# When attention's rows of weights begin, and when Q and K are loaded

## The chip, the cores and the metric

The kernel runs on one core of a Trainium2 chip. A core has TensorE (PE: matrix products and transposes, with its weight loads shown apart as PEld), VectorE (DVE), ScalarE (ACT), GpSimd (POOL) and SyncE (SP, which here issues all DMA transfers); each works off its own queue in order. The metric is the time on the device in microseconds, as the median over runs.

## The reference

One layer of a streaming encoder with 1024 tokens and 1024 channels, in float32. A combined projection gives Q, K and V for 8 heads of softmax attention and 8 heads of stick-breaking attention, and two gates. Each branch is projected, gated and summed; an output projection, a LayerNorm, a SwiGLU block of width 2816 and a second LayerNorm follow. What matters here is the attention:

```python
# a: softmax over own chunk and 8 previous ones (64 queries each), with a bias by distance
scores = einsum('bcqhd,bckhd->bhcqk', qc, kb) / sqrt(dh) + bias
out = einsum('bhcqk,bckhd->bcqhd', softmax(scores), vb)
# b: stick-breaking, strictly causal, 128 queries at a time
log_keep = where(causal, log_sigmoid(-z), 0.0)
suffix = cumsum(log_keep, axis=3, reverse=True) - log_keep
w = exp(where(causal, log_sigmoid(z) + suffix, -inf))
out = einsum('bhqs,bshd->bqhd', w, v)
```

Tokens are stored in reverse order, so that a query block's keys are its own block and those with higher numbers.

## The kernel before, in words

The stages come one after another: the combined projection, attention, the second branch's output projection and gating, the output projection with the first LayerNorm, and the two halves of the feed-forward block with the second LayerNorm. A matrix product in full precision is made of three products of rounded parts (a high part and the rest), which is why a tensor is "split" in many places: ACT writes the high part, DVE subtracts (lines 108 and 109).

Attention goes head by head, eight a heads (softmax, `br` 0), then eight b heads (stick-breaking, `br` 1). The queries of a head are eight blocks of 128, numbered 0 to 7, in two groups of four.

A **row** of weights is the work on one query block (a "unit" in the code). In an a head (`soft_block`) PE makes the scores, in pieces of up to 512 keys on two `sc` banks; DVE adds the bias and takes the minimum (line 492), ACT the exponential (497), DVE the reciprocal (499) and POOL the scaling (500). The rows of an a head reach over 5, 5, 5, 5, 4, 3, 2, 1 blocks of keys. In a b head (`stick_block`) ACT takes two sigmoids of each piece of scores (525, 526), DVE forms running products by scans (529, 533) and POOL multiplies (535). Its rows reach over 8, 7, 6, 5, 4, 3, 2, 1 blocks.

A **step** is one block of keys of one group: eight steps for the first group of a head and four for the second, twelve in all. In a step PE transposes the weights of that block for the queries of the group (the "turn", line 556) into one of three `tr` banks (in b heads one of the three holds an auxiliary tile, `ident_ps`, for the scans), ACT and DVE split them into `pt`, and two steps later (`LAG = 2`) PE multiplies them with V into the one `pv` bank (569, 570). After a group's last product ACT copies one half of the bank to `yt` and DVE adds the other (575, 576); only then can the next group's first product begin.

Between these, `fill_until` puts products of other work: gate projections (418) and the first branch's output projection (603), 18 products of 512 columns for each a head and 42 for each b head, spread over the twelve steps.

In the order in which the program is written, `LEAD[pos]` says how many rows, counted from the current head's first (eight per head), have begun by step `pos`; they are issued ahead of the step's turn. Before, the same twelve numbers held for both kinds of head. The head's Q and K (five transfers, in a heads also the bias row, an ACT pass and two small POOL writes) are loaded by `load_qk`, V by `load_v`; each has slots for two heads. At build time a planner orders each engine's instructions: by the order of the program, but what is not ready by its own costs gives way to later work that is. The order on the chip is the planner's and then fixed.

Of the kernel before, what the change touches and what calls it, by code (L numbers as in the profile page):

```python
# [31 lines left out]
LO, HI = slice(0, HW), slice(HW, 2 * HW)  # L32


LAG = 2
LEAD = (5, 6, 6, 7, 8, 8, 9, 10, 10, 11, 12, 13)

FILL = (18.0, 42.0)

# [7 lines left out]
def hybrid_trunk_kernel(ctx: ExitStack, tc, x, xt, w_in, b_gate, rel_bias, w_proj,  # L47
# [14 lines left out]
    def slot(tag, name, dtype=F32):  # L62
        return pool.tile([P, 1024], dtype, tag=tag, name=name, bufs=SLOTS[tag])
# [371 lines left out]
    def load_qk(hd):  # L435

        i, h = hd["i"], hd["h"]
        n = 2 * i + h
        q, k = (d[i][h * P:(h + 1) * P] for d in (q_dr, k_dr))
        for key, part in (("qs", None), ("kh", 0), ("kl", DH)):  # L440
            t = hd[key] = slot(key, f"{key}{n}", F32R)
            if part is None:
                dma(t.bitcast(F32), q)
            else:
                for half in (slice(0, DH), slice(DH, P)):
                    dma(t[half].bitcast(F32), k[part:part + DH])
        if hd["br"] == 0:
            hd["bias"] = rel_bias_tile(hd["n"])

    def load_v(hd):  # L450

        n = 2 * hd["i"] + hd["h"]
        t = slot("v", f"v{n}", F32R)
        dma(t.bitcast(F32), v_dr[n])
        hd["v"] = t.rearrange("p (t c) -> p t c", t=8)
# [16 lines left out]
    def rel_bias_tile(head):  # L472
        braw = slot("kp", f"braw{head}")
        src = rel_dr[head:head + 1, 0:640]
        dma(braw[:, 0:640],
            bass.AP(tensor=src.tensor, offset=src.offset, ap=[[1, P], [1, 640]]))
        bias = slot("kp", f"bias{head}")
        nc.scalar.activation(bias[:, 0:640], braw[:, 0:640][:, ::-1], AF.Copy, scale=-1.0)  # L478
        nc.gpsimd.memset(bias[0:DH, 576:640], BIG)  # L479
        nc.gpsimd.memset(bias[DH:P, 0:DH], BIG)  # L480
        return bias
# [158 lines left out]
    def fill_until(t):  # L640
        while state["t"] < t and not state["done"]:
            try:
                state["t"] += next(fill)
            except StopIteration:
                state["done"] = True


    heads = []
# [12 lines left out]
    wunits, vsteps = [], []  # L661
# [12 lines left out]
    wi = 0  # L674
# [2 lines left out]
    nhead = 12  # L677
    goal = 0.0
    load_qk(heads[0])
    load_v(heads[0])  # L680
    for si, (hd, g, st, box) in enumerate(vsteps):
        hidx, pos = si // nhead, si % nhead
        if hidx < 15 and pos == 1:
            load_qk(heads[hidx + 1])
        if hidx < 15 and pos == 4:
            load_v(heads[hidx + 1])
        while wi < min(hidx * 8 + LEAD[pos], len(wunits)):
            wunits[wi]()
            wi += 1
        if st == 0:  # L690
            steps_of[(hidx, g)] = value_steps(hd, g, box)
        turn, mult = steps_of[(hidx, g)][st]
        turn()
        last = goal
        goal += FILL[hd["br"]] / nhead
        fill_until(0.5 * (last + goal))
        pend.append(mult)
        if len(pend) > LAG:
            pend.pop(0)()
        fill_until(goal)  # L700
# [361 lines left out]
```

## Time and profile before

| | |
|---|---|
| median of 3 runs | 1499.21 us (1498.03 to 1502.22) |
| profiled execution | 1501.38 us |
| its span, first to last instruction | 1499.3 us |
| PE busy | 1440.3 us (96%) |
| DVE busy | 1043.9 us (70%) |
| ACT busy | 679.7 us (45%) |
| POOL busy | 282.4 us (19%) |
| granted TensorE clock, mean | 0.993 |

The profile gives, for one execution, each engine's busy time, the instructions in order of time with the idle time before each and what ended it, and sums of those waits. In a line of the timeline the first two numbers are start and length in microseconds, then engine, source line, operation, output and inputs; "x2" means that two neighbours of the same kind are merged. In a line of waits the numbers are the total in microseconds, how often, and the longest.

### The profile page before, as it was taken

How to read it: one execution, taken by the hardware profiler on the slowest of the kernel's cores; microseconds unless marked ns; L12 is line 12 of the kernel's file. 1: busy time of each engine (PE TensorE's matmuls, PEld its weight loads, DVE VectorE, ACT ScalarE, POOL GpSimd, SP SyncE). 2: the span in 40 equal slices, each digit the busy share in tenths (PEclk: the TensorE clock that was granted, in tenths of full speed). 3: DMA queues.
4: the chain of work that ended last, by engine and by line, in shares of the span. 5: the costliest groups of instructions: out<-in, count | busy, mean ns of one | idle time of the engine just before them, and what ended most of it. 6: DMA issues, size and time to landing. Idle time of an engine off the chain costs nothing. (4 is left out here: it accounts for less than half of the span.)

```text
span 1499.3 us, 19075 instructions
## 1 busy us (share of the span) xinstructions
PE 1440.3 (96%) x6728; PEld 1179.6 (79%) x6728; DVE 1043.9 (70%) x1702; ACT 679.7 (45%) x1174; POOL 282.4 (19%) x322
## 2 busy tenths in 40 slices
PE   8999999999999999899999899999999998999997
PEld 6788888887887777777787688888888886778886
DVE  8865556435878887887849966767777755767757
ACT  6444444336877778775303534444444433111201
POOL 0000000004344558650014000000000003341016
PEclk9999999999999999999999999999999999999999
DMA  6555555247754556647502123444444456677602
GB/s 211 163 175 169 168 168 170 98 144 213 206 170 142 159 165 204 187 157 280 183 0 87 62 100 121 152 155 155 155 155 154 155 189 232 245 249 267 234 8 105
DMA packets 81215, 244.05 MB, mean 163 GB/s; under 512 B 10064, under 2 KB 10064, under 8 KB 81120
## 3 DMA queue, kind: packets, MB, share of 16 engines
q1 hardware_dynamic: 81120, 242.84, 48.5%
q8 instruction: 53, 0.87, 0.2%
q14 instruction: 42, 0.34, 0.1%
HBM read 162.03 MB, written 80.77 MB: 162 GB/s over the span
## 5 line engine op out<-in xcount | busy, mean ns | idle before, releaser
L535 POOL TENSOR_TENSOR w_b<-w_b,kp_b 128x511 f32<-128x511 f32 (+3 forms) x96 | 97.5, 1021 | 51.5 <-DVE kp_b L533 40.6
L950 POOL TENSOR_TENSOR tda<-wdR,wdL 128x512 f32<-128x512 f32 x8 | 10.7, 1340 | 491.6 <-DMA wdR<-in_w_ffn_out_dram 477.8
L533 DVE TENSOR_TENSOR_SCAN kp_b<-kp_b,ident_ps 128x384 f32<-128x384 f32 (+6 forms) x88 | 78.3, 890 | 4.1
L479 POOL MEMSET bias<- 64x64 f32 x8 | 1.2, 146 | 334.5 <-ACT bias L478 334.5
L745 POOL TENSOR_TENSOR mv<-mv,neghalf 128x1 f32<-128x1 f32 x16 | 23.9, 1495 | 211.4 <-DVE mv L744 211.4
L525 ACT ACTIVATE kp_b<-sc_b 128x512 f32<-128x512 f32 (+3 forms) x96 | 48.5, 505 | 31.4 <-PE sc_b L462 26.5
L183 DVE TENSOR_TENSOR c<-sxp,c 128x512 f32<-128x512 f32 x16 | 11.1, 692 | 73.9 <-issue 40.7
L925 DVE TENSOR_TENSOR x<-dx,x 128x512 f32<-128x512 f32 x64 | 43.6, 689 | 24.6 <-PE dx L995 24.6
L109 DVE TENSOR_TENSOR pt_b<-tp_b,pt_b 128x512 fp32r<-128x512 f32 (+1 forms) x96 | 51.1, 543 | 10.9 <-ACT pt_b L108 10.4
L170 PE MATMUL szf<-x1S63h,wcf 128*128 128x512 f32 x176 | 57.8, 389 | 0.0
L500 POOL TENSOR_SCALAR w_a<-w_a,st_a 128x640 f32<-128x640 f32 (+2 forms) x64 | 42.6, 671 | 67.2 <-DVE st_a L499 49.6
L556 PE MATMUL tp_b<-ident,w_b 128*128 128x128 f32 x288 | 49.3, 277 | 5.2 <-DVE pt_b L109 2.8
L108 ACT CAST pt_b<-tp_b 128x512 fp32r<-128x512 f32 (+1 forms) x96 | 47.1, 497 | 13.7 <-PE tp_b L556 13.2
L109 DVE TENSOR_TENSOR sl<-h,sl 128x512 fp32r<-128x512 f32 x56 | 38.4, 686 | 20.2 <-ACT sl L108 20.2
L108 ACT CAST sl<-h 128x512 fp32r<-128x512 f32 x56 | 34.8, 621 | 35.6 <-PE syf L170 17.1
L109 DVE TENSOR_TENSOR pt_a<-tp_a,pt_a 128x512 fp32r<-128x512 f32 (+1 forms) x96 | 45.5, 484 | 7.6 <-ACT pt_a L108 7.3
L497 ACT ACTIVATE w_a<-w_a,st_a 128x640 f32<-128x640 f32 (+2 forms) x64 | 44.6, 698 | 12.8 <-DVE st_a L492 11.2
L118 PE MATMUL ops<-wh_o,ml 128*128 128x512 f32 x128 | 50.2, 392 | 0.2 <-DVE ml L109 0.2
L115 PE MATMUL ops<-wh_o,mh 128*128 128x512 f32 x128 | 50.2, 392 | 0.0
L116 PE MATMUL ops<-wl_o,mh 128*128 128x512 f32 x128 | 49.9, 390 | 0.0
L556 PE MATMUL tp_a<-ident,w_a 128*128 128x128 f32 x240 | 44.8, 277 | 5.0 <-POOL w_a L500 2.4
L833 ACT ACTIVATE h<-sxf 128x512 f32<-128x512 f32 x22 | 13.2, 598 | 79.6 <-PE sxf L170 79.6
(1881 smaller groups left out, 4833.4 us busy)
## 6 DMA issues: line engine op xcount, KB each, us to landing
s_dr<-sl SPq DMA_DIRECT2D x112, 256.0 KB, 2.2
sd<-s_dr SPq DMA_DIRECT2D x56, 512.0 KB, 5.2
wLf<-in_w_ffn_in_dram SPq DMA_DIRECT2D x22, 512.0 KB, 4.4
wRf<-in_w_ffn_in_dram SPq DMA_DIRECT2D x22, 512.0 KB, 3.6
wLp<-in_w_in_dram SPq DMA_DIRECT2D x17, 512.0 KB, 5.3
wRp<-in_w_in_dram SPq DMA_DIRECT2D x17, 512.0 KB, 4.0
v_dr<-v SPq DMA_DIRECT2D x16, 512.0 KB, 4.3
qs<-q_dr SPq DMA_DIRECT2D x16, 512.0 KB, 6.2
```

The costliest lines, as they stand in the source:

```text
L108: nc.scalar.copy(dst_h, src)
L109: nc.vector.tensor_tensor(dst_l, src, dst_h.bitcast(F32), ALU.subtract)
L115: mm(acc, lh, rh, start=(i == 0), stop=False)
L116: mm(acc, lh, rl, start=False, stop=False)
L118: mm(acc, ll, rh, start=False, stop=(i == n))
L170: mm(acc, lw[:, ks], rx, start=(first and kt == i == 0), stop=(kt == 3 and i == 2), skip_group_check=not first)
L497: nc.scalar.activation(s[:, 0:w], s[:, 0:w], AF.Exp, bias=st[:, m:m + 1], scale=-1.0, accum_out=st[:, 2:3])
L525: nc.scalar.activation(kp[:, c0:e], sc[:, 0:n], AF.Sigmoid, scale=-1.0)
L533: nc.vector.tensor_tensor_scan(kp[:, s0:e], kp[:, s0:e], ident_ps()[:, 0:e - s0], kp[:, s0 - 1:s0], ALU.mult, ALU.bypass)
L535: nc.gpsimd.tensor_tensor(be[:, m0:e], be[:, m0:e], kp[:, m0 - 1:e - 1], ALU.mult)
L556: tr(tp[:, (qb - lo_q) * P:(qb - lo_q + 1) * P], wt[qb - q0][:, (kb - qb) * P:(kb - qb + 1) * P], ident)
L925: nc.vector.tensor_tensor(dst, acc, dst, ALU.add)
```

## The change

The one list of twelve numbers becomes one list for a heads and one for b heads, chosen by the current head's kind. Counted in steps of a head, the rows of a head that begin in the head before (the first group's four and the first ones of the second) and in the head itself move as follows:

| row (block of queries) | 0 | 1 | 2 | 3 | 4 | 5 | 6 | 7 |
|---|---|---|---|---|---|---|---|---|
| begins before | step 6 of the head before | 7 | 9 | 10 | 11 | step 1 of its own head | 3 | 4 |
| now, under an a head | 2 | 4 | 6 | 8 | 10 | step 0 of its own head | 1 | 2 |
| now, under a b head | 2 | 4 | 6 | 8 | 10 | 11 of the head before | step 0 of its own head | 1 |

`load_qk` is written at step 8 for the head after the next, where it stood at step 1 for the next head; the second head's load moves ahead of the first head's `load_v`.

```diff
-LEAD = (5, 6, 6, 7, 8, 8, 9, 10, 10, 11, 12, 13)
+LEAD = ((6, 7, 9, 9, 10, 10, 11, 11, 12, 12, 13, 13), (7, 8, 9, 9, 10, 10, 11, 11, 12, 12, 13, 14))
 ...
     load_qk(heads[0])
+    load_qk(heads[1])
     load_v(heads[0])
     for si, (hd, g, st, box) in enumerate(vsteps):
         hidx, pos = si // nhead, si % nhead
-        if hidx < 15 and pos == 1:
-            load_qk(heads[hidx + 1])
+        if hidx < 14 and pos == 8:
+            load_qk(heads[hidx + 2])
         if hidx < 15 and pos == 4:
             load_v(heads[hidx + 1])
-        while wi < min(hidx * 8 + LEAD[pos], len(wunits)):
+        while wi < min(hidx * 8 + LEAD[hd["br"]][pos], len(wunits)):
             wunits[wi]()
             wi += 1
```

## The prediction

> **What bounds the kernel now.** I read the page's totals first, then busy time by stage, then the waits of TensorE (PE), then one head in order of time on PE, VectorE (DVE) and ScalarE (ACT).
>
> ```profile
> span 1499.3 us, 19075 instructions
> PE 1440.3 (96%) x6728; PEld 1179.6 (79%) x6728; DVE 1043.9 (70%) x1702; ACT 679.7 (45%) x1174; POOL 282.4 (19%) x322
> ```
>
> PE is busy 96% of the span, so the change can win only what PE idles in the stage it touches. Attention is that stage: softmax heads (called a) from 347.5 to about 474 us, stick-breaking heads (b) to 690. Columns: length of the stretch, then busy time of each engine.
>
> ```profile
> core 0: us, PE busy (x) PEld busy (x) DVE busy (x) ACT busy (x) POOL busy (x), PEclk, DMA share, GB/s
> 347.50:474.00 126.50, 120.62 (x732) 102.32 (x730) 98.64 (x357) 98.72 (x245) 50.72 (x81) 1.00 0.62 184
> 490.00:690.00 200.00, 185.90 (x997) 149.17 (x996) 162.80 (x272) 150.03 (x319) 117.30 (x152) 1.00 0.56 180
> ```
>
> PE idles 5.9 us in the a stretch and 14.1 us in the b stretch, at full granted clock. DVE is busy 81% in b (162.8 of 200): not the bound over a head, but possibly within one. PE's waits, first a, then the changeover with b:
>
> ```profile
> PE tp_a L556 <- POOL w_a L500: 2.4, 7, 0.8
> PE sc_a L461 <- DVE st_a L492: 2.1, 7, 0.8
> PE tp_a L556 <- DVE pt_a L109: 0.6, 3, 0.2
> PE pv_a L569 <- DVE yt L576: 0.4, 1, 0.4
> ```
>
> ```profile
> PE pv_b L569 <- DVE yt L576: 9.2, 11, 1.6
> PE tp_b L556 <- DVE pt_b L109: 2.8, 6, 0.7
> PE tp_a L556 <- DVE pt_a L109: 1.8, 3, 0.9
> PE tp_b L556 <- POOL w_b L535: 1.4, 2, 0.8
> ```
>
> Together 5.5 + 15.2 = 20.7 us. The largest item is the hand-over of the one pv bank between groups: the next group's first product waits until ACT and DVE have emptied it into yt. One such place on PE, ACT and DVE:
>
> ```profile
> 605.95 0.55 PE L556 MATMUL tp_b<-ident,w_b 128*128 128x128 f32 x3 [0.70 <-DVE pt_b L109]
> ...
> 608.51 0.40 PE L603 MATMUL yAps<-yl,wh_y 128*128 128x512 f32 x1
> 609.81 0.50 PE L569 MATMUL pv_b<-pt_b,v 128*128 128x512 f32 x1 [0.90 <-DVE yt L576]
> ```
>
> ```profile
> 607.16 0.59 ACT L575 COPY yt<-pv_b 64x512 f32<-64x512 f32 x1
> ```
>
> ```profile
> 599.45 0.42 DVE L529 TENSOR_TENSOR_SCAN kp_b<-kp_b,ident_ps 128x128 f32<-128x128 f32 x1 [0.50 <-ACT kp_b L525]
> 599.90 2.40 DVE L533 TENSOR_TENSOR_SCAN kp_b<-kp_b,ident_ps 128x384 f32<-128x384 f32 x2
> ...
> 603.13 0.41 DVE L529 TENSOR_TENSOR_SCAN kp_b<-kp_b,ident_ps 128x128 f32<-128x128 f32 x1
> 603.58 2.13 DVE L533 TENSOR_TENSOR_SCAN kp_b<-kp_b,ident_ps 128x256 f32<-128x256 f32 x2
> 605.63 0.86 DVE L109 TENSOR_TENSOR pt_b<-tp_b,pt_b 128x128 fp32r<-128x128 f32 x2
> 606.41 0.41 DVE L529 TENSOR_TENSOR_SCAN kp_b<-kp_b,ident_ps 128x128 f32<-128x128 f32 x1
> 606.85 1.86 DVE L533 TENSOR_TENSOR_SCAN kp_b<-kp_b,ident_ps 128x192 f32<-128x192 f32 x2
> 608.63 0.53 DVE L109 TENSOR_TENSOR pt_b<-tp_b,pt_b 128x384 fp32r<-128x384 f32 x1
> 609.08 0.67 DVE L576 TENSOR_TENSOR yt<-pv_b,yt 64x512 f32<-64x512 f32 x1
> ...
> 610.59 0.60 DVE L533 TENSOR_TENSOR_SCAN kp_b<-kp_b,ident_ps 128x192 f32<-128x192 f32 x1
> ...
> 611.42 0.87 DVE L533 TENSOR_TENSOR_SCAN kp_b<-kp_b,ident_ps 128x320 f32<-128x320 f32 x1
> ```
>
> ACT has its half by 607.75, but DVE begins its half only at 609.08: the scans of the six-block row (to 608.71) and a split of transposed weights stand before it. DVE runs without a gap from 599.45 on, because the four wide rows of the next head come in five steps. Emptied at once, the bank would be free at 607.75 + 0.67 = 608.42, before PE's last covering matmul begins (608.51). So the stalls here are DVE's backlog.
>
> **The change part by part.** No instruction is added or removed; rows of weights begin earlier, and loads move. The terms are taken against the profiled execution (1501.38 us, 2.1 outside its span), which lies 2.2 above the runs' median of 1499.21; I carry the sum over to the median.
>
> *Step table of b.* A head has 12 steps and takes about 25 us (200 us for 8 heads), so 2.1 us a step. Rows of 8, 7, 6, 5, 4, 3, 2, 1 blocks began at steps 6, 7, 9, 10, 11, 1, 3, 4; now at 2, 4, 6, 8, 10, 11, 0, 1. DVE pays for the first four 0.42 + 2.40 = 2.8, 0.41 + 2.13 = 2.5, 0.41 + 1.86 = 2.3 and, with the same first scan, 0.41 + 0.60 + 0.87 = 1.9 us. Before, these 9.5 us fell in steps 6 to 10, whose five steps give 10.5 us and must also hold the splits, a yt and the gA products. After, they spread over steps 2 to 9, eight steps or 16.8 us.
>
> ```profile
> L109 DVE TENSOR_TENSOR pt_b<-tp_b,pt_b 128x512 fp32r<-128x512 f32 x48 | 32.6, 680 | 3.0 <-ACT pt_b L108 2.6
> ...
> L533 DVE TENSOR_TENSOR_SCAN kp_b<-kp_b,ident_ps 128x128 f32<-128x128 f32 x8 | 3.8, 476 | 0.1
> ```
>
> *Hand-overs of the pv bank (9.2 us).* They are issued at steps 9 and 1. In front of step 9's stood the six-block row of that step; now step 9 has no row and step 8 a five-block one. In front of step 1's stood a three-block row; now a one-block and a two-block row (0.4 and, by the last row, 0.4 + 0.48 us). Bounds: all of it goes (-9.2), or none (0). The worked hand-over above leaves no wait once DVE is free, but some backlog will stay from step 8: I take -5.5, six tenths.
>
> *Turns that wait for a split (2.8 us in b).* A turn needs one of the two tr banks, freed by the split two turns earlier, and the splits wait behind scans as at 605.95. That cause shrinks in steps 8 to 10, but the 8- and 7-block rows now meet the four-block splits (0.68 us) of steps 2 to 4: DVE gets 2.8 + 0.7 + 0.7 + 2.5 + 0.7 = 7.4 us in three steps that give 6.3. PE is heavier there too, with wide scores, four transposes and two 512-column products a step, so it should be only a little ahead. Bounds: -2.8, and +17 if each of three wide rows in 8 heads costs a new 0.7. I take -0.8, since the sample head's own eight-block row at 599.45 delayed its next turns by nothing that the profile lists.
>
> *Rows that come late from GpSimd (POOL).* The fourth row of a head was issued two steps before the first turn that needs it, now four. Of 2.4 us in a, the longest, 0.8, is the first turn of all, which nothing precedes; the other 1.6 and b's 1.4 are this wait. Bounds -3.0 and 0; two more steps (2.1 us each in b) exceed every single wait, so I take -2.4.
>
> *Changeover from a to b (1.8 us).* Head 8's wide rows also spread over head 7's steps; bounds -1.8 and 0, I take -0.7, as DVE still pays the same scans there.
>
> *Scores in a (2.1 us).* Rows 7 and 8 now begin in the same step, three score pieces on two banks, while the other rows get an empty step between them. Bounds: -1.3 (all but the longest, 0.8, which is the start's) and +1.6 (one more wait per head of the typical (2.1 - 0.8) / 6 = 0.2). I take +0.5, near the loss.
>
> *Loads.* A load of Q and K is one transfer for Q and four for K; in a the bias row, its ACT flip and two POOL memsets come with it. All keep their number. The written place says little about when they start:
>
> ```profile
> 494.39 0.22 PE L461 MATMUL sc_b<-kh,qs 128*128 128x128 f32 x1
> ```
>
> ```profile
> 494.76 0.32 SPq L443 DMA_DIRECT2D qs<-q_dr  x1
> 495.13 1.10 SPq L446 DMA_DIRECT2D kh<-k_dr  x2
> 496.27 1.23 SPq L446 DMA_DIRECT2D kl<-k_dr  x2
> ```
>
> These five go out as soon as head 8's last row (128 columns) has read its Q and K: they are head 10's, written at step 1 of head 9, some 20 us later. The planner already pulls them to the moment the slot is free. With row 7 earlier that moment comes earlier too. So 0 in the steady state. At the start, head 1's loads (2.7 us of SP by these rows) pass V of head 0, and one more row precedes the first turn: between 0 and +1.2, I take +0.5.
>
> **Sum:** -5.5 - 0.8 - 2.4 - 0.7 + 0.5 + 0.5 = -8.4 us, so 1499.2 - 8.4 = 1490.8 us.
>
> **The rivals.**
> *The hand-over stays.* One pv bank remains, and if the product after it is only reordered, the 9.2 us stay and -2.9 is left: 1496.3. For it: both halves of emptying take 0.59 + 0.67 whatever comes first. Against it: DVE started 1.3 us after ACT ended. The Trainium skill (Perfetto Trace Analysis, Optimization Strategy) has the rule that the same gap repeating on the engine that should be full can mean too few buffers; by it this case holds. The trace does not bear it out well, since the wait varies with what DVE has in front.
>
> *Slower: the wide rows collide with the four-block splits.* Place: steps 2 to 6 of each b head. Price: 0.7 per wide row (the wait at 605.95), three rows, eight heads, +17; with my other terms kept (-7.6) that is +9.4, about 1508.6. It decides once such a row costs more than 7.6 / 24 = 0.32 us. For it: 7.4 us of DVE work in 6.3. Against it: step 3 and step 5 hold no row, and DVE enters step 2 without backlog.
>
> *More than listed.* If even pace removes every listed wait but the two longest of the start (0.8 each), 19 us vanish: 1480.
>
> **How the numbers follow.** About 0.3% (4.5 us) is what a measurement tells from no change. The forecast has 0.55, the bigger gain 0.05; the hand-over staying 0.20, which lies within 0.3%; the collision 0.20. So faster 0.60, same 0.20, slower 0.20. The forecast's own range is 1484 to 1495. Over all cases 1483 to 1504 leaves out about 0.2: half of the collision's chance, the bigger gain and small tails.
>
> **What would show it.** In PE's waits of the changed kernel: pv_b on yt below 4 us; tp on POOL below 1.5 besides the start; tp_b on pt_b at 2 to 3 us. In DVE's order at a hand-over, yt right behind ACT's copy, with at most one split before it. The stretch of b heads shorter by 6 to 8 us, a by 1 to 2, and every stage outside attention unchanged within 1 us. Q and K should go out right after their predecessors' last row, now two steps sooner in an a head and three (6 us) in a b head. Wrong would be: new waits of turns on pt_b in steps 4 to 6, as long as those that went; the pv waits unchanged; or a stage outside attention that moves.

## The result and the profile after

The changed kernel takes 1491.56 us in the median (1489.66 to 1494.44), the kernel before 1499.80 (1498.03 to 1502.22) beside it. The ratio is 0.9948, with an interval of 0.9934 to 0.9961. A later comparison gave 1491.45 against 1501.63, ratio 0.9934 (0.9918 to 0.9949). The forecast was 1490.8. The profiled execution took 1494.44 us.

The page's totals of the changed kernel:

```profile
span 1492.7 us, 19082 instructions
PE 1440.3 (96%) x6728; PEld 1184.2 (79%) x6728; DVE 1046.4 (70%) x1702; ACT 681.9 (46%) x1176; POOL 282.8 (19%) x322
```

PE and DVE do almost exactly what they did before. For attention by stage, I cut each trace at the first score and at the start of the last addition into yt of the a heads and of the b heads. Busy time in each stretch, first before, then changed:

```profile
347.50:492.60 145.10, 137.09 (x816) 114.16 (x814) 115.32 (x387) 115.10 (x283) 64.56 (x101) 1.00 0.60 178
492.60:686.30 193.70, 179.71 (x966) 144.68 (x967) 158.33 (x265) 146.42 (x312) 115.57 (x151) 1.00 0.55 176
```

```profile
347.50:497.20 149.70, 140.29 (x828) 118.34 (x827) 118.76 (x391) 120.05 (x288) 67.10 (x104) 0.99 0.60 170
497.20:677.60 180.40, 174.71 (x956) 143.69 (x957) 156.98 (x262) 143.36 (x308) 114.13 (x148) 1.00 0.60 191
```

Attention ends 8.7 us earlier (686.3 to 677.6), and 6.9 us of that is idle time of PE: 8.0 + 14.0 = 22.0 us before, 9.4 + 5.7 = 15.1 us after. The two stretches don't share it. b is 13.3 us shorter and a is 4.6 longer. Of these 4.6 us, 3.2 are busy time of PE: twelve more matmuls now stand ahead of the cut, and some run at half clock (last section). The other 1.4 us is idle time, which did grow in a.

PE's waits after, first from 347 to 474 us, then from 460 to 690 (what it waited for: total, times, longest):

```profile
PE pv_a L570 <- DVE yt L577: 3.0, 6, 0.8
PE sc_a L463 <- DMA kl<-k_dr: 2.1, 1, 2.1
PE sc_a L462 <- DVE st_a L493: 1.6, 5, 0.4
```

```profile
PE tp_b L557 <- DVE pt_b L110: 3.6, 6, 1.6
PE pv_b L570 <- DVE yt L577: 1.8, 4, 0.7
PE tp_a L557 <- DVE pt_a L110: 1.6, 3, 0.8
PE pv_a L570 <- DVE yt L577: 0.4, 2, 0.2
```

The big one, the hand-over of pv in b, fell from 9.2 to 1.8 us. Waits for rows from POOL (2.4 + 1.4) are gone. In their place stand 3.0 us at the hand-over in a, where 0.4 stood, and one wait of 2.1 us for a load.

One b hand-over of the changed kernel, at nearly the place the prediction worked out, on PE, ACT and DVE:

```profile
604.93 0.40 PE L604 MATMUL yAps<-yl,wh_y 128*128 128x512 f32 x1
605.39 0.50 PE L570 MATMUL pv_b<-pt_b,v 128*128 128x512 f32 x1
```

```profile
604.04 0.59 ACT L576 COPY yt<-pv_b 64x512 f32<-64x512 f32 x1
```

```profile
602.19 0.67 DVE L110 TENSOR_TENSOR pt_b<-tp_b,pt_b 128x512 fp32r<-128x512 f32 x1
603.10 0.56 DVE L110 TENSOR_TENSOR pt_b<-tp_b,pt_b 128x384 fp32r<-128x384 f32 x1 [0.24 <-ACT pt_b L109]
603.75 0.69 DVE L607 TENSOR_TENSOR gA<-yAps,gA 128x512 f32<-128x512 f32 x1
604.65 0.68 DVE L577 TENSOR_TENSOR yt<-pv_b,yt 64x512 f32<-64x512 f32 x1 [0.22 <-ACT yt L576]
```

Before, DVE began its half 1.3 us after ACT had ended. Now DVE is there first and waits 0.22 us for ACT. The bank is empty at 605.33, the covering product ends at 605.33, and the next group's first product starts at 605.39 with no wait listed.

Later stages: from the last yt of b to the end it is 813.0 us before and 815.1 in this profile, but 813.0 again in the second profile of the same kernel. That difference is not the change's; the granted clock over this stretch averages 0.98 in the slower profile and 0.99 in the two others.

### The profile page after: what moved, and what is told of

Read it like the earlier page. It is cut to its first block, busy times and chain, and to the rows that moved or that the text cites. A ratio compares the mean times of both kernels' runs of the same rounds, so it can differ in the third digit from the quotient of the medians.

```text
span 1492.7 us, 19082 instructions
## 1 busy us (share of the span) xinstructions
PE 1440.3 (96%) x6728; PEld 1184.2 (79%) x6728; DVE 1046.4 (70%) x1702; ACT 681.9 (46%) x1176; POOL 282.8 (19%) x322
## 5 line engine op out<-in xcount | busy, mean ns | idle before, releaser
L527 ACT ACTIVATE w_b<-sc_b 128x511 f32<-128x511 f32 (+3 forms) x96 | 48.6, 506 | 0.0
```

Source lines behind the costliest of these rows:

```text
L527: nc.scalar.activation(be[:, m0:e], sc[:, m0 - c0:n], AF.Sigmoid)
```

## The experiments

Each is an edit of the kernel before, whose line numbers its rows have, unless said otherwise. `OLD` is the list before, `NA` and `NB` the changed lists of a and b.

**The parts one by one.** Four kernels, timed together against 1500.94 us.

Only b's list is new:

```diff
-LEAD = OLD              # one list for both kinds
+LEAD = (OLD, NB)         # a heads, b heads
```

> Only the b heads' list of the change, loads and a heads as before. If DVE's burst of scans in b is what the change removes: 6 to 8 us faster than the kernel before, PE's pv_b waits on yt fall from 9.2 us to under 3, the a stretch unchanged (about 5.9 us idle). If the gain belongs to the a heads or the loads: within 2 us of before.

Measured: 1488.56 us, ratio 0.9920 (0.9903 to 0.9937). PE's waits of this kernel from 490 to 690 us:

```profile
PE tp_b L556 <- DVE pt_b L109: 3.5, 5, 1.6
PE pv_b L569 <- DVE yt L576: 1.8, 4, 0.7
```

These are the changed kernel's waits in b. So b's list alone gives 12.4 us, more than the whole change and more than the 6 to 8 us that I expected. The listed waits don't explain all of it: from the last addition of the a heads to that of the b heads PE idles 5.0 us instead of 14.0, and its busy time falls from 179.7 to 176.0 us for the same matmuls but one (966 and 965). Why those count as shorter is not shown. On another chip it gave 1488.08, ratio 0.9912 (0.9895 to 0.9930):

> The b list alone once more: 12 us faster than before, 2 to 4 us faster than the changed kernel if the a list and the moved loads together cost something.

Only a's list is new:

```diff
+LEAD = (NA, OLD)
```

> Only the a heads' list of the change. By the theory the waits on POOL w_a in a (2.4 us) go, but as many new ones on yt come (3.0 us in the changed kernel): between 2 us faster and 1 us slower than before. If a heads carried the gain: 4 us faster or more.

Measured: 1501.93 us, ratio 1.0004 (0.9994 to 1.0013). Its waits from 347 to 474 us show the trade:

```profile
PE pv_a L569 <- DVE yt L576: 3.2, 7, 0.8
PE sc_a L461 <- DVE st_a L492: 1.6, 5, 0.3
PE tp_a L556 <- POOL w_a L500: 0.8, 1, 0.8
```

The wait for POOL goes from 2.4 to 0.8, the start's own, and the waits of scores fall by 0.5. The hand-over in a grows by 2.8 us instead. a's list alone is worth nothing.

Both lists, loads as before:

```diff
+LEAD = (NA, NB)
```

> Both lists, loads as before. If the loads' place says little, as the planner pulls them to the moment their slot is free: within 2 us of the changed kernel (8 us faster than before). If the earlier rows need the earlier loads: clearly slower than the changed kernel, with PE waits on DMA of K or Q in many heads.

Measured: 1491.23 us, ratio 0.9932 (0.9915 to 0.9949). That is 2.7 us above b's list alone, with intervals that overlap.

Only the loads move:

```diff
+    load_qk(heads[1])        # ahead of load_v(heads[0])
-        if hidx < 15 and pos == 1:
-            load_qk(heads[hidx + 1])
+        if hidx < 14 and pos == 8:
+            load_qk(heads[hidx + 2])
```

> Only the moved loads, the list as before. If their place says little: within 2 us of before, and the Q transfers of the steady state within 1 us of their time before. If loading ahead carries gain by itself: 3 us faster or more.

Measured: 1499.63 us, ratio 0.9991 (0.9981 to 1.0001). The moved loads by themselves are worth nothing that can be told. Nor do the transfers move: in the last five b heads that of Q starts 4.1 to 5.1 us after ACT's copy of the hand-over at step 1, in this kernel and in the one before alike. The whole change once more, timed with b's list alone and two kernels below against 1501.63:

> The changed kernel once more, on the same chip as the two below: 8 to 9 us faster than before. If the wait on the transfer of K at the start (2.1 us) belongs to the moved loads, it is there again.

Measured: 1491.45, 10.2 us below before, where 8 to 9 was expected, and 3.4 us above b's list alone (1488.08); the wait at the start is there again. Twice, then, the lists of both kinds came out some 3 us behind b's list alone, with intervals that overlap each time. The profiles would put it elsewhere: attention, cut as above, takes 325.4 and 328.1 us in two profiles of b's list alone, 326.3 with both lists and the old loads, and 330.1 and 330.6 in two of the whole change, which alone has the wait and the slow clock at its start (last section). Whether a's list, or the loads together with the lists, takes something back is not settled.

**Why the hand-over in b waited.** The theory was DVE's backlog of scans. The rival was the single bank: whatever stands in front of DVE, the hand-over costs the same. This kernel keeps the old list and the one bank, and leaves scans out of DVE's queue, so that its output is no longer the layer's:

```diff
-            if s0 < e:
+            if s0 < e and c0 == 0:
```

> The kernel before, but in b heads the scan of the second piece of the rows over 5 to 8 blocks is left out (some 4.6 us of DVE work a head, so part of the stick-breaking weights is not computed); the order of the rows stays bunched and the pv bank stays single. DVE's burst as the cause: pv_b waits on yt fall from 9.2 us to under 3, and the kernel is 8 to 13 us faster. The single bank as the cause: the 9.2 us stay and the gain is under 4 us.

Measured: 1490.34 us against 1501.02, ratio 0.9919 (0.9899 to 0.9939). Its waits in b:

```profile
PE pv_b L569 <- DVE yt L576: 2.1, 8, 0.5
PE tp_b L556 <- DVE pt_b L109: 0.8, 2, 0.5
```

With the rows where they were and the bank as it was, the wait falls from 9.2 to 2.1 us. At the hand-overs of step 9 in the first seven b heads DVE now starts 0.03 us after ACT has ended, where it started 0.9 to 1.7 us after it; PE's order of work in b is that of before but for a handful of products. The backlog is the cause. Spreading the scans and removing some of them bring nearly the same time.

Is the exact step decisive? The same even spacing, one step later, so that the six-block row stands at step 7 and the five-block row meets the hand-over at step 9:

```diff
+LEAD = (OLD, (6, 7, 8, 9, 9, 10, 10, 11, 11, 12, 12, 13))
```

> The b list one step later throughout (a heads and loads as before): the wide rows just as evenly spaced, now at steps 3, 5, 7, 9, so that the five-block row stands at the hand-over's own step 9. If only the density of scans matters: within 2 us of the kernel with the b list alone (1488.6). If what stands in front of the hand-over matters: pv_b waits on yt back at 4 us or more, and 3 to 6 us slower than that kernel.

Measured: 1489.17 us, ratio 0.9916 (0.9900 to 0.9932). Waits in b:

```profile
PE pv_b L569 <- DVE yt L576: 5.6, 12, 0.8
PE tp_b L556 <- DVE pt_b L109: 1.9, 4, 0.6
```

The hand-over's wait came back in good part (5.6 us), as the backlog theory says, but turns waited less (1.9 for 3.5) and the time is within 1 us of b's list alone. The loss of 3 to 6 us that I expected did not come. What gains is the even pace; of the two places tried, one step apart, neither is measurably better.

The prediction's slower rival, wide rows that meet the four-block splits, at full density: the four wide rows in steps 2, 3, 4 and 5.

```diff
+LEAD = (OLD, (7, 8, 9, 10, 11, 12, 12, 12, 12, 12, 13, 14))
```

> The b list with the four wide rows at steps 2, 3, 4, 5, as bunched as before but well ahead of the hand-over; a heads and loads as before. If a burst costs wherever it stands: turns wait on pt_b for 8 us or more (3.5 with the even list) and the gain over the kernel before shrinks from 12 us to under 6. If the place alone matters: within 2 us of the kernel with the b list alone.

Measured: 1502.08 us, ratio 1.0005 (0.9991 to 1.0019). Waits in b:

```profile
PE tp_b L556 <- DVE pt_b L109: 14.4, 19, 1.4
PE pv_b L569 <- DVE yt L576: 0.9, 3, 0.4
```

Here the hand-overs are freer than in the changed kernel (0.9 for 1.8), and the whole gain is gone all the same: 19 turns wait 14.4 us for a split, in most heads those of two blocks and of one block (steps 6 and 7), just behind the burst. The rival's mechanism is real. With an empty step between the wide rows it does not set in.

**The hand-over in a.** One such place in the changed kernel, on PE, ACT and DVE:

```profile
450.02 0.28 PE L571 MATMUL pv_a<-pt_a,v 128*128 128x128 f32 x1
...
452.76 0.50 PE L570 MATMUL pv_a<-pt_a,v 128*128 128x512 f32 x1 [0.74 <-DVE yt L577]
```

```profile
450.10 0.83 ACT L498 ACTIVATE w_a<-w_a,st_a 128x640 f32<-128x640 f32 x1 [0.54 <-DVE st_a L493]
450.83 0.18 ACT L498 ACTIVATION_READ_ACCUMULATOR w_a<-w_a,st_a 128x1 f32 x1
450.93 0.46 ACT L109 CAST pt_a<-tp_a 128x384 fp32r<-128x384 f32 x1
451.41 0.58 ACT L576 COPY yt<-pv_a 64x512 f32<-64x512 f32 x1
```

```profile
452.02 0.69 DVE L577 TENSOR_TENSOR yt<-pv_a,yt 64x512 f32<-64x512 f32 x1
```

PE's last product of the group ends at 450.30, but ACT copies only at 451.41: the five-block row's exponential, which a's new list puts at step 8, is in ACT's queue just before the copy. DVE's half follows at 452.02. The kernel before has no row at step 8, and at the same hand-over its copy starts 0.19 us after the product's end at 447.53, with the next exponential behind it:

```profile
447.22 0.48 ACT L108 CAST pt_a<-tp_a 128x384 fp32r<-128x384 f32 x1 [0.50 <-PE tp_a L556]
447.72 0.58 ACT L575 COPY yt<-pv_a 64x512 f32<-64x512 f32 x1
448.33 0.83 ACT L497 ACTIVATE w_a<-w_a,st_a 128x640 f32<-128x640 f32 x1
```

Here it is ACT's order that sets the hand-over. Three such waits (0.74, 0.77 and 0.74 us) make 2.25 of the 3.2 us; at two of the four smaller ones (0.31 and 0.19) DVE began 0.5 to 0.6 us after ACT. A list for a that keeps wide rows away from steps 8 and 9, with b's new list and the old loads:

```diff
+LEAD = ((6, 7, 8, 9, 9, 10, 11, 12, 12, 12, 13, 14), NB)
```

> The b list of the change with a third list for a heads: rows at steps 3, 5, 6, 7, 10, 11, 1, 2, so none at steps 8 and 9 in front of the hand-over, and the first group's last row five steps ahead; loads as before. If a's new waits come from rows in front of the hand-over and its old ones from the late last row: both go, 1 to 3 us faster than the kernel with the b list alone (1488.6). If a heads are at PE's limit anyway: within 1 us of it.

Measured: 1487.24 us, ratio 0.9905 (0.9876 to 0.9935), 1.3 us below b's list alone (1488.56). Once more on another chip:

> The b list with the third list for a heads once more: 13 us faster than before and about 1 us faster than the b list alone, if a rows kept clear of the hand-over are worth anything.

Measured: 1487.06, ratio 0.9906 (0.9889 to 0.9922), 14.6 us below before. Its waits in a (347 to 474), then in b:

```profile
PE pv_a L569 <- DVE yt L576: 1.3, 6, 0.3
PE sc_a L461 <- DVE st_a L492: 0.7, 4, 0.2
PE tp_a L556 <- POOL w_a L500: 0.2, 1, 0.2
```

```profile
PE pv_b L569 <- DVE yt L576: 2.0, 5, 0.6
PE tp_b L556 <- DVE pt_b L109: 1.9, 2, 1.6
```

The hand-over in a costs 1.3 us instead of 3.0, and this has the lowest median of the study, 4.4 us below the changed kernel in the same comparison (1487.06 against 1491.45; the intervals just touch). Against b's list alone (1488.08) the 1.0 us is inside both intervals, so whether a better list for a is worth anything is not settled.

One long wait stays in b in the kernels that have b's new list, 1.6 us in the last head, where the split of a projection's weights also stands on DVE. This kernel adds to the last one:

```diff
-            w = load_proj(1, c // 2, "op", nc.vector)
+            w = load_proj(1, c // 2, "op", nc.gpsimd if n == 0 else nc.vector)
```

> The b list with the third list for a heads, and besides the first weight of the second branch's output projection is split by POOL instead of DVE. In the last b head that split on DVE stands before a turn's split (the longest remaining wait, 1.6 us). If DVE's queue is still what is left: that wait goes and this is 1 to 2 us faster than the same kernel without it. If POOL's slower split comes too late for the projection: no gain or up to 2 us slower.

Measured: 1489.26 us, ratio 0.9918 (0.9901 to 0.9936), not better. A wait of 1.38 us stayed, and DVE shows why:

```profile
644.97 0.44 PE L556 MATMUL tp_b<-ident,w_b 128*128 128x128 f32 x2 [1.38 <-DVE pt_b L109]
```

```profile
642.27 0.42 DVE L529 TENSOR_TENSOR_SCAN kp_b<-kp_b,ident_ps 128x128 f32<-128x128 f32 x1 [1.84 <-ACT kp_b L525]
642.73 1.60 DVE L533 TENSOR_TENSOR_SCAN kp_b<-kp_b,ident_ps 128x192 f32<-128x192 f32 x2
644.25 1.37 DVE L109 TENSOR_TENSOR pt_b<-tp_b,pt_b 128x512 fp32r<-128x512 f32 x2
```

DVE first idles 1.84 us for ACT's half of a row, then runs that row's scans to 644.25, and only then the splits. The weight split was not in the way: in the kernel without this edit it starts at 647.32, behind the split that the turn waits for (646.73). My suspicion was wrong.

## Why the prediction was right or wrong

The total was right: 1490.8 forecast, 1491.56 measured, 8.4 us of gain against 8.2. The mechanism of its largest term was right too. The other terms were not as good as their sum, and that the sum met the time so closely is in part luck.

- **Hand-overs of pv in b: forecast -5.5, measured -7.4** (9.2 to 1.8). Mechanism right, size too small. I kept four tenths for the backlog of step 8's row; the worked hand-over above shows no backlog at all. The missing-scan kernel confirms the cause.
- **Turns that wait for a split: forecast -0.8, measured +0.8** (2.8 to 3.6). Wrong sign, small. One wait of 1.6 us in the last head is the longest part of the 3.6; there DVE had first idled 1.94 us for ACT.
- **Rows late from POOL: forecast -2.4, measured -3.8.** They go entirely, the start's 0.8 included, which I had kept, so the total lies outside the bound of -3.0.
- **Changeover: forecast -0.7, measured -0.2** (1.8 to 1.6).
- **Scores in a: forecast +0.5, measured -0.5** (2.1 to 1.6). The two waits of the start (0.84 and 0.30) are gone, though, and that hides a small loss: the wait in each later head grew from 0.18 to 0.31, which is the loss the term was for.
- **The start: forecast +0.5, at most +1.2; the profile shows a wait of 2.1** and a slower clock behind it (last section).
- **A term that the prediction did not have: the hand-over of pv in a, +2.8** (0.4 to 3.2 in all). The wait stands in the prediction's list with 0.4 us, and I gave it no term. I looked at which row meets the hand-over on DVE in b, and never asked the same of ACT in a. This is the step that failed.

These seven come to -6.2 us of listed waits, and turns in a that no longer wait for a split (0.6) to -6.8, beside the 6.9 us of idle time that the stretches show. PE's busy time, 316.8 to 315.0 over both, makes the rest of the 8.7; the prediction has no term for it. Errors cancelled: gains put too low (the hand-over in b by 1.9, the rows from POOL by 1.4, the scores by 1.0) come to 4.3 us, and losses left out or put too low (the hand-over in a 2.8, the turns 1.6, the start 1.6, the changeover 0.5) to 6.5.

Of the signs named, pv_b below 4 us, no POOL waits, and yt right behind ACT's copy came as said. Turns on pt_b, 3.6 us, lie above the 2 to 3 that was named. Measured from ACT's copy at the hand-over of step 1, Q's transfers start 5.3 to 6.7 us sooner in the last five b heads, where 6 was named, and 1.0 to 2.8 us sooner in the last six a heads. The stretches did not come as said: b is 13.3 shorter where 6 to 8 stood, a 4.6 longer where 1 to 2 shorter stood, 3.2 of it busy time and 1.4 from a's new waits.

The rival that the hand-over stays falls. The Trainium skill (Perfetto Trace Analysis, Optimization Strategy) reads the same gap repeating on the engine that should be full as possibly too few buffers; here the wait went from 9.2 to 1.8 and 2.1 us in two kernels with the one bank unchanged. The collision is a real mechanism (14.4 us of turns), but not at this change's spacing. Its deciding point was 0.32 us a row: the changed kernel's 3.6 us over 24 wide rows is 0.15, and the burst, whose 14.4 us over 32 rows is 0.45, has lost the gain.

## What to carry to other kernels

A stall at the hand-over of a single buffer is first a question of order: look at what the engines that empty it have queued in front. Spacing the long instructions evenly won 12 us here without a new buffer, and packing them elsewhere lost all of it again. Ask it of every engine that has a part in the hand-over (in a it was ACT), and test each part of a change alone: one list gave the gain, the other two parts gave nothing.

## What the runs showed of the hardware

**A short wait halved the clock.** In the changed kernel the low part of head 1's K is issued at 351.28. PE comes to it at 358.86, 7.6 us later, and can use it only at 361.00. PE, SP, and then busy time and granted clock (the column after POOL's) in four stretches of 3.41 us:

```profile
361.00 0.75 PE L463 MATMUL sc_a<-kl,qs 128*128 128x320 f32 x2 [2.14 <-DMA kl<-k_dr]
```

```profile
351.28 1.09 SPq L447 DMA_DIRECT2D kl<-k_dr  x2
```

```profile
354.32:357.73 3.41, 3.30 (x20) 2.81 (x21) 2.31 (x14) 3.41 (x12) 2.54 (x4) 1.00 0.99 182
357.73:361.14 3.41, 1.27 (x9) 0.94 (x8) 0.62 (x3) 0.69 (x2) 0.67 (x3) 1.00 1.04 198
361.14:364.55 3.41, 3.41 (x15) 3.33 (x16) 2.11 (x8) 1.54 (x3) 0.00 (x0) 0.50 1.01 200
364.55:367.96 3.41, 3.41 (x25) 3.15 (x25) 2.99 (x14) 2.28 (x8) 1.61 (x2) 1.00 1.03 201
```

After a stretch in which PE was busy 37%, the granted clock is 0.50 for one stretch of 3.41 us, which costs some 1.7 us beside the 2.1 of the wait. The Trainium skill (TensorE: Matmul & The Clock Gate, What's actually happening) has half rate after an idle window of some 3.4 us; the half rate agrees, but here the stretch before it was not idle, and a gap of 2.1 us in it was enough. What decides the step down seems to be PE's busy share in such a stretch: in these profiles the clock changes only at multiples of 3.41 us from its first change. In attention, half rate also followed stretches of that grid with PE busy 26% (this kernel's second profile), 45% (the start of the kernel without the scans, half rate for 6.8 us), and 46 and 49% (the last b head, in the second profiles of the list that keeps clear and of b's list alone); with 52 and 53% at that same place, in the profiles of both lists and of b's list alone, the clock stayed full. The limit is near a half and not sharp: in later stages three stretches with 48 to 50% kept the full clock. So what a wait of this length costs depends on where in the grid it falls. The second profile of this kernel has the same wait (2.51 us); those of both lists with old loads, and of the loads alone, do not have it. Whether the timed executions pay it stays open: the medians with moved loads (1491.45, 1491.56) and without (1491.23) are alike.

**Table loads multiplied at the changeover.** ACT, before, loaded its function table once between a and b. In the changed kernel:

```profile
473.67 1.28 ACT L526 ACT_TABLE_LOAD   x1
475.58 1.28 ACT L498 ACT_TABLE_LOAD   x1
477.39 1.28 ACT L527 ACT_TABLE_LOAD   x1
```

The last exponential of the last a head and the first row of the first b head now begin close together, and the order interleaves them: two more loads, 2.6 us of ACT. With b's list alone there is one load, with a's changed list three, with the list that keeps clear of steps 8 and 9 one. PE hardly feels it: the turns of the last a head wait 1.6 us with three loads (changed kernel) and 1.8 with one (b's list alone).
